# Denser idle products, eight packed first rows, and first-query banks copied whole by ScalarE with their rotation later

## The chip, the cores and the metric

The kernel runs on one core of a Trainium2 chip. It is timed by the device time of one execution, in microseconds; the time before the change is the median of three runs. TensorE is called PE here, its weight loads PEld, VectorE DVE, ScalarE ACT, GpSimd POOL, and SyncE, which issues most of the transfers, SP. L221 means line 221 of the kernel before.

## The reference, cut to what matters

One layer of an encoder on 256 tokens of width 2048, in float32. Only the first projection and the differential attention that reads it are touched by the change:

```python
h = rms_norm(x, norm_mix_pre[l])
proj = jnp.einsum('bsd,dc->bsc', h, w_in[l])
qa, ka, va, qn, kn, vn, gates = jnp.split(proj, split_at, axis=-1)
qa = apply_rope(qa.reshape(B, S, DA_HEADS, 2, DA_HEAD_DIM), cos, sin)
ka = apply_rope(ka.reshape(B, S, DA_HEADS, 2, DA_HEAD_DIM), cos, sin)
...
oa = diff_attention(qa, ka, va, lam)
```

After it come a neighbourhood attention, gates, an output projection and a squared-ReLU MLP of width 8192, which take up most of the time and which the change leaves as they are.

## The kernel before

**Numbers in two parts.** Each float32 operand is split in a high part, rounded to the type float32r that PE multiplies in one pass, and a low part, the rest. ACT makes the high part with a cast or a copy, DVE the low part with a subtraction (`split`, L137 and L143 for the casts, L145 for the subtraction). `wgroup` multiplies the high part of a weight tile with both parts of the activations (a product of 512 columns: 256 tokens high, 256 low; L221), and its low part with the high tokens alone (256 columns, L223). `agroup` takes three products of 512 columns for the same (L264 to L266).

**Groups.** The 2048 rows of `w_in` are 16 row tiles of 128, taken in four chunks of four. A group is 512 columns of `w_in`: four PSUM banks of 128 columns each for queries and keys (`wgroup`, one bank for each `b`), two banks for values (`agroup`). The first three groups are qa (queries), ka (keys) and va (values) of the first half of the heads. The eight banks of PSUM are two pools of four; qa, ka and va take theirs in turn from the same four, so bank `b` of ka can start only when bank `b` of qa has been read, and va needs the first two of ka.

**The start.** Four tiles `near` hold one row of the weights and of the transposed x each, side by side in a packed host array `front`, one transfer for each. The products of chunk 0 are issued row by row: four high ones, then four low ones (`k_first`). Chunks 1 to 3 come as pairs of rows, `first_w` and `xT` in turn, with casts and subtractions of two rows at a time; their products are left to the scheduler. `x_part` (L304, L305) scales the transposed x by the gains of the norm and splits it into `hT`. Before the data there are nine products of ones with ones into a bank that nobody reads (L171).

**The end of a query group.** `rope_evac` takes a bank by `halves`: ACT copies the right half (L289, to `rope_r`), DVE adds the left half of the bank to it (L291, to `rope_s`). Then DVE rotates with four more instructions and two products with the tables in `pack` (`cosT`, `sinT`; L432 to L435), ACT casts the high part (L418) and DVE subtracts for the low one (L419).

**The scale of the rows.** The projection is taken of x times gains, and the factor 1/rms of each token comes later. `second(ch)` runs between the chunks of ka: it loads four tiles of x in rows, ACT squares them and sums (L339, eight instructions), DVE and POOL make `rx` of the sums (L345, L98, L103), DVE puts it on a diagonal (`rxb_d`, L90), PE spreads it over the partitions (L91), ACT copies the result to `rxb` (L92), and DVE multiplies it into the tables (L349, L350). From there on rotated keys carry the factor.

**What sets the order.** A scheduler places the instructions of each engine by its own model of time, under the dependencies and the orders that `issue_after` adds; each engine then works through its list in that order. Transfers are issued by SP in order, at most eight under way at a time, since the ninth waits for the first. Weight tiles rotate through three buffers each for raw, high and low; a transfer into a raw buffer waits until the tile before in it has been split.

Of the kernel before, what the change touches and what calls it, by code (L numbers as in the profile page):

```python
# [17 lines left out]
P = 128  # L18
# [11 lines left out]
NMM = 4  # L30

# [19 lines left out]
def encoder_layer(ctx: ExitStack, tc: tile.TileContext, a, out):  # L51
# [55 lines left out]
    last_load = [None]  # L107
    front = []
    scaled = [None]

    def load(src, k0, nk, c0, cw, name):

        raw = wp.tile([P, nk, cw], F32, tag="raw", name=f"{name}_w")
        view = src[k0 * P : (k0 + nk) * P, c0 : c0 + cw].rearrange("(k p) c -> p k c", p=P)
        last_load[0] = nc.sync.dma_start(raw, view).ins
        return raw

    def split(raw, name, pieces=2, after=(), then=None):
# [7 lines left out]
        for s in range(pieces):  # L126
# [14 lines left out]
            with tc.issue_after(front[0]) if listed else nullcontext():  # L141
                if listed:
                    front[0] = nc.scalar.copy(hi[part], src).ins  # L143
                with tc.issue_after(front[1]) if then else nullcontext():
                    sub = nc.vector.tensor_sub(lo[part], src, hi[part].bitcast(F32)).ins  # L145
                if then:
                    front[1] = sub
# [7 lines left out]
    near = [page([P, (0 if k else KD) + 512 + T], F32, f"near{k}") for k in range(4)]  # L155
# [12 lines left out]

    idle = bank("idle")
    for i in range(9):  # L170
        nc.tensor.matmul(idle[:, :P], ones, ones, start=True, stop=True)  # L171

    xT = [None] + [page([P, 4, T], F32, f"xT{i}") for i in range(1, 4)]
# [38 lines left out]
    def wgroup(src, c0, act, nk, evac, name, first=(), hook=None, mid=None, after={}, k_first=False, inner=None):  # L212
# [14 lines left out]
        for ch in range(nk // 4):  # L227
# [3 lines left out]
            if ch < len(first):  # L231
                w = split(
                    first[ch], f"{name}_{ch}", 4 if k_first and ch == 0 else 2,
# [4 lines left out]
            if k_first and ch == 0:  # L238
# [47 lines left out]
    def halves(ps, name):  # L286

        r = t1k(f"{name}_r")
        act = nc.scalar.copy(r, ps[:, T:]).ins  # L289
        s = t1k(f"{name}_s")  # L290
        halved.extend((act, nc.vector.tensor_add(s, ps[:, :T], r).ins))  # L291
# [7 lines left out]
    def x_part(k):  # L299

        src = xT[k // 4][:, k % 4] if k > 3 else near[k][:, 512:]
# [27 lines left out]
    def x_rows(i):  # L329
        xt = page([P, 2, 512], F32, f"x_{i}")  # L330
        nc.sync.dma_start(
            xt, a["x"].rearrange("(t p) c -> p t c", p=P)[:, :, i * 512 : (i + 1) * 512]
        )
        xp.append(xt)
# [53 lines left out]
    halved = []  # L388
# [10 lines left out]
    def second(ch):  # L399
        if ch == 1:  # L400
            late[1] = halved[:8]
        if ch == 2:
            for i in range(4):
                x_rows(i)
# [22 lines left out]

    def rope_evac(dst):
        def evac(b, ps):
            s = halves(ps, "rope")  # L430
            u = t1k("rope_u")
            nc.vector.tensor_mul(u[0:64], s[64:128], sinT[64:128])  # L432
            nc.vector.tensor_mul(u[64:128], s[0:64], sinT[0:64])
            nc.vector.tensor_mul(s, s, cosT)
            nc.vector.tensor_add(s, s, u)  # L435
            parts(dst, (slice(None), b), s)
# [181 lines left out]
    for kind in ("a", "n"):  # L618
        for half in range(2):
# [6 lines left out]
            wgroup(w_in, qc + off, hmov, KD, qev(qT), f"q{nm}", **(head if nm == "a0" else {}))  # L626
            wgroup(w_in, kc + off, hmov, KD, kev(kT), f"k{nm}", **(head_k if nm == "a0" else {}))
            agroup(w_in, vc + off, hstat, KD, v_evac(v), f"v{nm}")
# [742 lines left out]
def _host_arrays(inputs):  # L1371
# [34 lines left out]
    w = arr["w_in"][: 4 * P, QA : QA + 512].reshape(4, P, 512)  # L1406
    arr["front"] = np.concatenate(
        [f["norm_mix_pre"][0].reshape(KD, P).T]
        + [part for k in range(4) for part in (w[k], arr["xT"][:, k])],
# [20 lines left out]
```

## Time and profile before

| | |
|---|---|
| median of three runs | 1341.35 us (1341.18 to 1341.43) |
| profiled execution, its own time | 1341.7 us |
| its span, first to last instruction | 1339.9 us |
| instructions | 16240 |
| granted PE clock over the span | 0.998 |
| first product on real data | 5.14 us after the span's start |
| first product of the key group ka | 28.70 us |
| first product of the value group va | 52.19 us |

Rows of the timeline give start, duration, engine, line, operation, output and inputs, shapes and a count; rows that follow each other alike are merged. What stands in brackets is how long the engine had been idle and what ended it. A PE row shows the whole way of a product through the array, so that rows overlap: the distance of two starts is what a product costs.

### The profile page before, as it was taken

How to read it: one execution, taken by the hardware profiler on the slowest of the kernel's cores; microseconds unless marked ns; L12 is line 12 of the kernel's file. 1: busy time of each engine (PE TensorE's matmuls, PEld its weight loads, DVE VectorE, ACT ScalarE, POOL GpSimd, SP SyncE). 2: the span in 40 equal slices, each digit the busy share in tenths (PEclk: the TensorE clock that was granted, in tenths of full speed). 3: DMA queues.
4: the chain of work that ended last, by engine and by line, in shares of the span. 5: the costliest groups of instructions: out<-in, count | busy, mean ns of one | idle time of the engine just before them, and what ended most of it. 6: DMA issues, size and time to landing. Idle time of an engine off the chain costs nothing.

```text
span 1339.9 us, 16240 instructions
## 1 busy us (share of the span) xinstructions
PE 1328.2 (99%) x6306; PEld 1112.9 (83%) x6306; DVE 1076.7 (80%) x1246; ACT 732.3 (55%) x864; POOL 38.5 (3%) x71
## 2 busy tenths in 40 slices
PE   9999999999999999999999999999999999999997
PEld 8888888888888888888888888888888888888885
DVE  7978866667777887655788999999988988898886
ACT  6655555544545554444476666666555555555542
POOL 0000000000000000000100000000000000000000
PEclk9999999999999999999999999999999999999999
DMA  9874655564565656575658777877797998698995
GB/s 343 277 219 161 197 166 179 184 186 157 188 220 171 209 192 209 199 277 188 223 187 275 239 249 277 294 237 249 250 360 291 401 374 336 247 372 333 354 355 201
DMA packets 116028, 335.85 MB, mean 251 GB/s; under 512 B 16752, under 2 KB 17008, under 8 KB 115952
## 3 DMA queue, kind: packets, MB, share of 16 engines
q1 hardware_dynamic: 96560, 266.13, 58.3%
q10 hardware_dynamic: 12672, 43.00, 8.3%
q0 software_dynamic: 6720, 25.69, 4.9%
q8 instruction: 49, 0.80, 0.2%
q14 instruction: 27, 0.22, 0.0%
HBM read 307.01 MB, written 29.61 MB: 251 GB/s over the span
## 4 chain that ended last, share of the span: by engine, by line
PE 96%; DMA 1%; DVE 1%; ACT 0%; SPq 0%; issue 0%; DVEq 0%; POOLq 0%; POOL 0%; ACTq 0%
PE u L740 25%; PE p L740 24%; PE ga L740 6%; PE gb L740 6%; PE ba L740 3%; PE bb L740 3%; PE qn_p L221 2%; PE kn_p L221 2%; PE y_p L266 2%; PE y_p L265 2%; PE y_p L264 2%; PE ka_p L221 2%; PE qn_p L223 1%; PE kn_p L223 1%; PE qa_p L221 1%; PE vn_p L264 1%
## 5 line engine op out<-in xcount | busy, mean ns | idle before, releaser
L145 DVE TENSOR_TENSOR y_l<-y_w,y_h 128x1024 fp32r<-128x1024 f32 x32 | 37.9, 1222 | 30.3 <-ACT y_h L137 30.3
L137 ACT CAST y_h<-y_w 128x1024 fp32r<-128x1024 f32 x32 | 32.0, 1051 | 40.1 <-PE y_p L266 32.5
L264 PE MATMUL y_p<-y_h,mh 128*128 128x512 f32 x128 | 50.1, 391 | 0.0
L265 PE MATMUL y_p<-y_l,mh 128*128 128x512 f32 x128 | 49.9, 390 | 0.0
L266 PE MATMUL y_p<-y_h,ml 128*128 128x512 f32 x128 | 49.8, 390 | 0.0
L221 PE MATMUL qn_p<-hT,qn_h 128*128 128x512 f32 x128 | 45.9, 400 | 0.0
L221 PE MATMUL ka_p<-hT,ka_h 128*128 128x512 f32 x128 | 45.4, 399 | 0.3 <-DVE rope_s L291 0.3
L221 PE MATMUL kn_p<-hT,kn_h 128*128 128x512 f32 x128 | 45.4, 398 | 0.0
L221 PE MATMUL qa_p<-hT,qa_h 128*128 128x512 f32 x128 | 43.6, 399 | 0.7 <-DVE hT L305 0.7
L740 PE MATMUL u<-u_2h,h2T 128*128 128x512 f32 x128 | 44.0, 396 | 0.0
L740 PE MATMUL u<-u_1h,h2T 128*128 128x512 f32 x128 | 43.4, 390 | 0.0
L740 PE MATMUL u<-u_4h,h2T 128*128 128x512 f32 x128 | 43.2, 391 | 0.0
L740 PE MATMUL u<-u_7h,h2T 128*128 128x512 f32 x128 | 41.0, 389 | 0.0
L740 PE MATMUL u<-u_6h,h2T 128*128 128x512 f32 x128 | 41.0, 389 | 0.0
L223 PE MATMUL qn_p<-hT,qn_l 128*128 128x256 f32 x128 | 35.9, 281 | 0.0
L223 PE MATMUL kn_p<-hT,kn_l 128*128 128x256 f32 x128 | 35.7, 280 | 0.0
L223 PE MATMUL ka_p<-hT,ka_l 128*128 128x256 f32 x128 | 35.2, 281 | 0.0
L223 PE MATMUL qa_p<-hT,qa_l 128*128 128x256 f32 x128 | 32.4, 281 | 0.3 <-DVE qa_l L145 0.3
L221 PEld LDWEIGHTS ka_p<-hT,ka_h 128*128 128x128 f32 x128 | 23.8, 188 | 6.0 <-DVE rope_s L291 0.7
L221 PEld LDWEIGHTS qn_p<-hT,qn_h 128*128 128x128 f32 x128 | 24.1, 188 | 5.3
L221 PEld LDWEIGHTS kn_p<-hT,kn_h 128*128 128x128 f32 x128 | 24.0, 188 | 5.3
L740 PEld LDWEIGHTS u<-u_1h,h2T 128*128 128x128 f32 x128 | 24.0, 188 | 5.0
(1473 smaller groups left out, 4422.2 us busy)
## 6 DMA issues: line engine op xcount, KB each, us to landing
y_w<-in_w_out SPq DMA_DIRECT2D x16, 1024.0 KB, 5.3
bh<-keeph ACTq DMA_DIRECT2D x30, 512.0 KB, 9.3
bl<-keepl ACTq DMA_DIRECT2D x30, 512.0 KB, 11.0
keeph<-ah POOLq DMA_DIRECT2D x18, 512.0 KB, 3.7
keepl<-al POOLq DMA_DIRECT2D x18, 512.0 KB, 7.1
va_w<-in_w_in SPq DMA_DIRECT2D x8, 1024.0 KB, 5.2
qn_w<-in_w_in SPq DMA_DIRECT2D x8, 1024.0 KB, 5.1
kn_w<-in_w_in SPq DMA_DIRECT2D x8, 1024.0 KB, 5.1
```

Of the source, the lines that this page charges most:

```text
L137: nc.scalar.copy(hi[part], src)
L145: sub = nc.vector.tensor_sub(lo[part], src, hi[part].bitcast(F32)).ins
L221: nc.tensor.matmul(ps[b], hi[:, k % 4, cs], mv, start=(k == 0), stop=False)
L223: nc.tensor.matmul(ps[b][:, :T], lo[:, k % 4, cs], mv[:, :T], start=False, stop=(k == nk - 1))
L264: nc.tensor.matmul(ps[t], sh, hi[:, k % 4], start=(k == 0), stop=False)
L265: nc.tensor.matmul(ps[t], sh, lo[:, k % 4], start=False, stop=False)
L266: nc.tensor.matmul(ps[t], sl, hi[:, k % 4], start=False, stop=(k == nk - 1))
L740: ins = nc.tensor.matmul(self.ps[i], st, mv[:, blk], start=i not in self.begun, stop=last and n == 2).ins
```

## The change

It has three parts. The idle products read a tile `warm` that DVE fills, in float32r and 512 columns wide, ten of them. Eight rows instead of four are packed into `front` and taken row by row (`NEAR`), and the transfers of chunk 1 fall away. The banks of the first queries (qa of the first half alone) are copied whole by ACT to four tiles `rope_c`; the add of the halves and the rotation are put into a list `rotations`, from which `second` takes two each at chunks 2 and 3 of ka, behind the low part of the last split so far. The casts of ka's chunk 1 are ordered behind these copies instead of behind the eight instructions of `halves`, and the loads of va behind the x rows.

```diff
+NEAR = 8
@@ load @@
-        last_load[0] = nc.sync.dma_start(raw, view).ins
+        with tc.issue_after(rows_load[0]) if rows_load[0] else nullcontext():
+            last_load[0] = nc.sync.dma_start(raw, view).ins
@@ split @@
+                last_low[0] = sub
...
-    near = [page([P, (0 if k else KD) + 512 + T], F32, f"near{k}") for k in range(4)]
+    near = [page([P, (0 if k else KD) + 512 + T], F32, f"near{k}") for k in range(NEAR)]
...
+    warm = page([P, 512], F32R, "warm")
+    nc.vector.memset(warm.bitcast(F32), 1.0)
     idle = bank("idle")
-    for i in range(9):
-        nc.tensor.matmul(idle[:, :P], ones, ones, start=True, stop=True)
+    for i in range(10):
+        nc.tensor.matmul(idle, warm[:, :P], warm, start=True, stop=True)
...
-    first = [[n[:, :512] for n in near]]
-    for i in range(1, 4):
+    first = [[n[:, :512] for n in near[i : i + 4]] for i in range(0, NEAR, 4)]
+    for i in range(NEAR // 4, 4):
@@ wgroup @@
-            if k_first and ch == 0:
+            if k_first and ch < NEAR // 4:
@@ second @@
         if ch == 1:
-            late[1] = halved[:8]
+            late[1] = copied
+        if ch > 1:
+            for _ in range(2):
+                rotations.pop(0)()
@@
+    def rope(dst, b, s):
+        u = t1k("rope_u")
+        nc.vector.tensor_mul(u[0:64], s[64:128], sinT[64:128])
+        nc.vector.tensor_mul(u[64:128], s[0:64], sinT[0:64])
+        nc.vector.tensor_mul(s, s, cosT)
+        nc.vector.tensor_add(s, s, u)
+        parts(dst, (slice(None), b), s)
...
+    def rope_late(dst):
+        def evac(b, ps):
+            c = t2k(f"rope_c{b}")
+            copied.append(nc.scalar.copy(c, ps.rearrange("p (a b) -> p a b", a=2)).ins)
+
+            def rest():
+                s = t1k("rope_s")
+                with tc.issue_after(last_low[0]):
+                    nc.vector.tensor_add(s, c[:, 0], c[:, 1])
+                rope(dst, b, s)
+
+            rotations.append(rest)
+
+        return evac
...
+            q_evac = rope_late(qT) if nm == "a0" else qev(qT)
```

The lists of the engines change in three places that the prediction speaks of. The first is DVE's list from the last split of the first keys' chunk 0 (`ka_0`) on; `qa_p` are banks of the first queries, `ka_n_l` low parts of chunk n of ka. Before:

```order
L145 TENSOR_TENSOR ka_0_l<-first_k_w,ka_0_h 128x1024 x2
L291 TENSOR_TENSOR rope_s<-qa_p_146,rope_r 128x256
L432 TENSOR_TENSOR rope_u<-rope_s,pack 64x256
L433 TENSOR_TENSOR rope_u<-rope_s,pack 64x256
L291 TENSOR_TENSOR rope_s<-qa_p_147,rope_r 128x256
```

With the change:

```order
L149 TENSOR_TENSOR ka_0_l<-first_k_w,ka_0_h 128x1024 x2
L149 TENSOR_TENSOR ka_1_l<-ka_1_w,ka_1_h 128x1024 x2
L463 TENSOR_TENSOR rope_s<-rope_c_326 128x256
L149 TENSOR_TENSOR ka_2_l<-ka_2_w,ka_2_h 128x1024
L441 TENSOR_TENSOR rope_u<-rope_s,pack 64x256
L442 TENSOR_TENSOR rope_u<-rope_s,pack 64x256
L463 TENSOR_TENSOR rope_s<-rope_c_336 128x256
```

Both subtractions of ka's chunk 1 now stand ahead of the first rotation, which reads ACT's copy and no bank. The second place is ACT's list between the casts of ka's chunk 2 and the end of the squares (`jx` are the squares, `x_...` the rows of x, `le` the exponentials of lambda, `qa` the high part of a rotated query). Before:

```order
L137 CAST ka_2_h<-ka_2_w 128x1024 x2
L418 CAST qa_140<-rope_s 128x256
L339 ACTIVATE jx_516,ssx<-x_467 128x512
L339 ACTIVATE jx_518,ssx<-x_467 128x512
L418 CAST qa_140<-rope_s 128x256
L339 ACTIVATE jx_520,ssx<-x_469 128x512
L339 ACTIVATE jx_522,ssx<-x_469 128x512
L137 CAST ka_3_h<-ka_3_w 128x1024 x2
L339 ACTIVATE jx_524,ssx<-x_471 128x512
```

With the change:

```order
L141 CAST ka_2_h<-ka_2_w 128x1024 x2
L141 CAST ka_3_h<-ka_3_w 128x1024 x2
L429 CAST qa_145<-rope_s 128x256 x2
L346 ACTIVATE jx_525,ssx<-x_458 128x512
L346 ACTIVATE jx_527,ssx<-x_458 128x512
L429 CAST qa_145<-rope_s 128x256
L346 ACTIVATE jx_529,ssx<-x_460 128x512
L429 CAST qa_145<-rope_s 128x256
L346 ACTIVATE jx_531,ssx<-x_460 128x512
L346 ACTIVATE jx_533,ssx<-x_462 128x512
```

All four casts of rotated queries now stand among the first squares, where before the last of them stood behind all eight. The third place is DVE's list at the change from keys to values (`va_n_l` are low parts of va's chunk n, `ka_p` banks of the keys). Before:

```order
L357 TENSOR_REDUCE ls<-lv 128x2
L145 TENSOR_TENSOR va_0_l<-va_0_w,va_0_h 128x1024
L90 TENSOR_SCALAR rxb_d_538<-ident,rx 128x128
L90 TENSOR_SCALAR rxb_d_541<-ident,rx 128x128
L348 TENSOR_SCALAR rxs<-rx 128x2
L145 TENSOR_TENSOR va_0_l<-va_0_w,va_0_h 128x1024
L419 TENSOR_TENSOR qa_141<-rope_s,qa_140 128x256
L360 SCALAR_TENSOR_TENSOR lam<-le 128x1
L145 TENSOR_TENSOR va_1_l<-va_1_w,va_1_h 128x1024 x2
L291 TENSOR_TENSOR rope_s<-ka_p_385,rope_r 128x256
```

With the change:

```order
L364 TENSOR_REDUCE ls<-lv 128x2
L367 SCALAR_TENSOR_TENSOR lam<-le 128x1
L91 TENSOR_SCALAR rxb_d_547<-ident,rx 128x128
L91 TENSOR_SCALAR rxb_d_550<-ident,rx 128x128
L355 TENSOR_SCALAR rxs<-rx 128x2
L298 TENSOR_TENSOR rope_s<-ka_p_358,rope_r 128x256
L149 TENSOR_TENSOR va_0_l<-va_0_w,va_0_h 128x1024 x2
L356 TENSOR_TENSOR pack<-pack,rxb 128x256
L357 TENSOR_TENSOR pack<-pack,rxb 128x256
L149 TENSOR_TENSOR va_1_l<-va_1_w,va_1_h 128x1024
L441 TENSOR_TENSOR rope_u<-rope_s,pack 64x256
L442 TENSOR_TENSOR rope_u<-rope_s,pack 64x256
```

The low parts of va's first two chunks moved behind the row scale and the first key bank. On PE the two products of the row scale (`rxb_p`) moved from the middle of ka's chunk 3 to its end; SP's list is the same but for the packed rows and one small input that is issued two transfers later. Some DVE and ACT instructions of the down projection trade places with a neighbour.

More of the change, by code (lines that the diff above doesn't have):

```diff
@@ L107, in encoder_layer @@
     last_load = [None]
+    last_low = [None]
+    rows_load = [None]
     front = []
@@ L232, in wgroup @@
                 w = split(
-                    first[ch], f"{name}_{ch}", 4 if k_first and ch == 0 else 2,
+                    first[ch], f"{name}_{ch}", 4 if k_first and ch < NEAR // 4 else 2,
                     then=(lambda k: x_part(ch * 4 + k)) if k_first else None,
@@ L299, in x_part @@
     def x_part(k):
-        src = xT[k // 4][:, k % 4] if k > 3 else near[k][:, 512:]
+        src = xT[k // 4][:, k % 4] if k >= NEAR else near[k][:, 512:]
         d = hT[k // 2][:, k % 2]
@@ L387, in encoder_layer @@
     first_k = []
-    halved = []
+    rotations = []
+    rows = []
     def tables():
```

33 lines of the change are left out of this document (15 added, 18 removed).

## Prediction

> **What bounds the kernel now.** I read the page's busy times and its chain first, then the list of who waits for whom on TensorE (PE), then the timeline of the first 75 us.
>
> ```profile
> PE 1328.2 (99%) x6306; PEld 1112.9 (83%) x6306; DVE 1076.7 (80%) x1246; ACT 732.3 (55%) x864; POOL 38.5 (3%) x71
> ...
> PE 96%; DMA 1%; DVE 1%; ACT 0%; SPq 0%; issue 0%; DVEq 0%; POOLq 0%; POOL 0%; ACTq 0%
> ```
>
> ```profile
> PE idle L171 <- POOL ones L163: 1.0, 1, 1.0
> PE qa_p L221 <- DVE hT L305: 0.7, 2, 0.5
> PE qa_p L223 <- DVE qa_l L145: 0.3, 1, 0.3
> PE ka_p L221 <- DVE rope_s L291: 0.3, 1, 0.3
> ```
>
> PE sets the end, and these are all its waits in 1340 us (total, times, longest). The change keeps every real product, so it can only remove what these waits cost and must not make new ones. The timeline (start, duration, engine) gives their price, because a pipelined PE row hides part of a wait.
>
> ```profile
> 5.14 1.17 PE L221 MATMUL qa_p<-hT,qa_h 128*128 128x512 f32 x4 [0.51 <-DVE hT L305]
> ...
> 8.01 1.09 PE L221 MATMUL qa_p<-hT,qa_h 128*128 128x512 f32 x4
> 8.94 0.63 PE L223 MATMUL qa_p<-hT,qa_l 128*128 128x256 f32 x4
> 9.41 1.09 PE L221 MATMUL qa_p<-hT,qa_h 128*128 128x512 f32 x4
> ...
> 11.14 1.19 PE L221 MATMUL qa_p<-hT,qa_h 128*128 128x512 f32 x4 [0.17 <-DVE hT L305]
> ...
> 12.68 0.39 PE L223 MATMUL qa_p<-hT,qa_l 128*128 128x256 f32 x1 [0.34 <-DVE qa_l L145]
> ...
> 28.70 0.40 PE L221 MATMUL ka_p<-hT,ka_h 128*128 128x512 f32 x1
> ...
> 32.94 0.86 PE L221 MATMUL ka_p<-hT,ka_h 128*128 128x512 f32 x3
> 34.11 0.50 PE L221 MATMUL ka_p<-hT,ka_h 128*128 128x512 f32 x1 [0.31 <-DVE rope_s L291]
> 34.44 0.28 PE L223 MATMUL ka_p<-hT,ka_l 128*128 128x256 f32 x1
> ```
>
> The wait at 5.14 is for the first transfer and stays. An undisturbed row of the weights (four high, four low products) takes 9.41 - 8.01 = 1.40 us, its four high ones 0.93 (0.233 each). So 11.14 is 9.41 + 1.40 + **0.33**; 12.68 is 11.14 + 0.93 + **0.61**; 34.11 is 32.94 + 3 x 0.233 + 0.47, and the product behind it starts 0.10 late: **0.57**. All that the change can save is 0.33 + 0.61 + 0.57 = 1.51 us, 0.11% of the run.
>
> **Idle products.** Ten float32r products of 512 columns replace nine float32 ones of 128 (two passes each), and wait for a DVE memset instead of POOL's.
>
> ```profile
> 0.74 0.20 POOL L163 MEMSET ones<- 128x128 f32 x1 [0.29 <-POOLq L1420]
> ...
> 1.00 2.72 PE L171 MATMUL idle<-ones 128*128 128x128 f32 x11 [1.00 <-POOL ones L163]
> ...
> 4.02 0.61 PE L171 MATMUL idle<-ones 128*128 128x128 f32 x4
> ```
>
> Eleven passes take 2.72 us, 0.25 each, the last four 0.61, 0.15 each with one row's tail in both: PE's pace about doubles near 3.9 us, 2.9 after the first pass and before the real work at 5.14. No row shows a DVE memset of 128x512; bounds are 0.20 (POOL's, a quarter of the size) and 0.69 (DVE's two-input 128x512, below). I take 0.5, nearer to the row of the same engine and size: first idle product at 1.3, some six at twice 0.233 until 3.9, four at 0.233, end about 5.0. Cost 0; the ends are -0.1 and +0.2 us at 5.14. "VectorE: DVE Perf Modes" of the Trainium skill (Zero memsets can be issued as uint32) says that a memset takes a cycle per element whatever its type; at 0.96 GHz that is an estimate of 0.53 us, and the sum stays.
>
> **Packed rows.** The bytes ahead of each row are the same, and ScalarE's waits show them landing.
>
> ```profile
> 7.78 0.51 ACT L304 ACTIVATE hT<-near,near 128x256 fp32r<-128x256 f32 x1 [0.29 <-DMA near<-in_front]
> ...
> 8.84 0.69 DVE L145 TENSOR_TENSOR qa_l<-near,qa_h 128x512 fp32r<-128x512 f32 x1
> ...
> 9.11 1.05 ACT L137 CAST qa_h<-first_w 128x1024 fp32r<-128x1024 f32 x1 [0.31 <-DMA first_w<-in_w_in]
> ...
> 11.36 1.05 ACT L137 CAST qa_h<-first_w 128x1024 fp32r<-128x1024 f32 x1 [0.39 <-DMA first_w<-in_w_in]
> ```
>
> Between 7.78 and 9.11 land 512 KB, until 11.36 another 768 KB. A packed row is 384 KB: row 4 lands near 8.8, then 9.9, 11.0, 12.1. From 7.78 to the end of its low half at 9.53 row 3 needs 1.75 us. So row 4 is complete at 10.5, and PE wants it at 10.8; rows 5 to 7 at 11.7, 12.8, 13.9 against 12.2, 13.6, 15.0. Both waits of chunk 1 go: **-0.94 us** (at the ends 0 and -0.94; chunk 2's lows are then due with some 0.1 us to spare, which I leave in the range). The eight rows cost ScalarE and DVE a few more short instructions, each hidden in these leads.
>
> **Banks emptied by ScalarE.** Four 128x512 copies replace four 128x256 ones; DVE's add moves off the bank. Their price lies between the rows of half the size and of a 128x512 activation out of a bank:
>
> ```profile
> 28.11 0.37 ACT L289 COPY rope_r<-qa_p 128x256 f32<-128x256 f32 x1 [1.32 <-DVE rope_s L291]
> ...
> 71.50 0.69 ACT L459 ACTIVATE va<-va_p,rx 128x512 fp32r<-128x512 f32 x1 [0.73 <-PE va_p L266]
> ```
>
> I take 0.6, near the second, which has the size. The fourth copy starts when the q products end, at 27.8 (28.70 - 0.94 is the first k product). Bank 3 is wanted 3 x 4 x 0.35 = 4.2 us later: the third wait goes, **-0.57 us**. Behind this copy stand the casts of ka_1, from 28.4.
>
> **What is late next: the v group.** Its low weights were early only because DVE never paused:
>
> ```profile
> 27.60:49.80 22.20, 21.89 (x127) 18.86 (x126) 21.86 (x43) 17.54 (x36) 0.71 (x1) 1.00 0.96 322
> ```
>
> ```profile
> 25.32 2.36 DVE L145 TENSOR_TENSOR ka_l<-first_k_w,ka_h 128x1024 fp32r<-128x1024 f32 x2 [0.22 <-ACT ka_h L137]
> ...
> 27.60 0.42 DVE L291 TENSOR_TENSOR rope_s<-qa_p,rope_r 128x256 f32<-128x256 f32 x1
> ...
> 33.97 1.22 DVE L145 TENSOR_TENSOR ka_l<-ka_w,ka_h 128x1024 fp32r<-128x1024 f32 x1
> ...
> 47.53 2.35 DVE L145 TENSOR_TENSOR va_l<-va_w,va_h 128x1024 fp32r<-128x1024 f32 x2
> ...
> 52.19 0.40 PE L264 MATMUL va_p<-va_h,hT 128*128 128x512 f32 x1
> ...
> 54.92 0.39 PE L264 MATMUL va_p<-va_h,hT 128*128 128x512 f32 x1
> ```
>
> DVE is busy for 21.86 of 22.20 us (third busy figure of the window), and va_1's lows end at 49.88. Afterwards DVE pauses twice. First, both halves of ka_1_l now stand ahead of all rotations: DVE is done with ka_0 at 27.68 and waits for ka_1_h until 29.5, 1.8 us. Second, ScalarE's queue puts the casts of rotated queries ahead of the squares of x, and each needs DVE's last add of that rotation.
>
> DVE from 29.5 to the fourth rotation's last add: six subtractions at 1.13 (2.35 less 1.22) and 22 short ones at 0.40 (sixteen between 27.60 and 33.97), 6.8 + 8.8 = 15.6, so 45.1. Three squares are done by then.
>
> ```profile
> 40.49 0.64 ACT L339 ACTIVATE jx<-x 128x512 f32<-128x512 f32 x1
> ...
> 42.34 0.62 ACT L339 ACTIVATE jx<-x 128x512 f32<-128x512 f32 x1
> ...
> 43.80 0.16 DVE L345 TENSOR_REDUCE sx<-ssx 128x2 f32<-128x8 f32 x1
> ...
> 44.31 0.71 POOL L103 TENSOR_TENSOR rx<-rx_m,expo 128x2 f32<-128x2 f32 x1 [42.86 <-DVE rx_m L98]
> 45.53 0.48 DVE L90 TENSOR_SCALAR rxb_d<-ident,rx 128x128 f32<-128x128 f32 x2
> 45.99 1.22 DVE L145 TENSOR_TENSOR va_l<-va_w,va_h 128x1024 fp32r<-128x1024 f32 x1
> ```
>
> Cast 0.4, five squares at 0.62 (three take 42.34 - 40.49): 48.6; it was 43.0. DVE, with nothing else ahead in its queue, has waited 2.5 us. The row scale takes 45.02 - 43.80 = 1.2 to POOL's end, rxb_d and rxs 0.46, the first k bank's add 0.34: 50.75. Then va_0_l 2.3, two table products 0.7, va_1_l's first half 1.1, two short ones 0.9, its second half 1.2: **57.0 us**. PE meets that operand at its 20th v product, in the run of before at 52.19 + 19 x 0.228 (54.92 - 52.19 is twelve) = 56.5; without new waits now 55.0. Waits for va_0_l, va_1_l and the row scale come to 2.0 us together. Later low weights keep 1 us and more (va_2 is due after 63.5, done near 61), so nothing is added behind it.
>
> **Sum** against the profiled execution, 1341.7 us (span 1339.9): -0.94 - 0.57 + 2.0 = +0.5 us, 1342.2. The three runs' median, 1341.35, lies 0.35 below it, so I forecast 1341.9, between 1341.2 and 1342.8.
>
> **Late swaps.** The order differs again in the down products, by one DVE step of 1.2 to 2.3 us:
>
> ```profile
> L694 DVE TENSOR_TENSOR d080el<-d080t,d080eh x2: 1219/1220/1220, 1098.5 to 1101.8; 128x1024 fp32r<-128x1024 f32 x2
> ...
> L740 PE MATMUL p<-d080el,bh x4: 389/389/389, 1106.9 to 1108.9; 128*128 128x512 f32 x4
> ```
>
> The second half is done at 1103.0 and used from 1106.9; this lead of 3.9 us hides the swap. Without it the swap would cost at most 2.3 us a step.
>
> **Rivals.** (1) The gain stays. If DVE's short steps and ScalarE's squares run 2 us ahead of my chain, v never waits: 1341.35 - 1.5 = 1339.9. For it: some thirty estimated steps in a row, and a 5 to 7 us lead before. Against: both queue orders are fixed, and DVE had no slack.
> (2) The clock, ending slower. If the idle block does not bring the pace up by 5.14, real products run at half pace. Price: before, the change came 2.9 us after the first idle product; counted again from 5.14 that loses 1.45 us, and the v chain, which hangs on the fourth copy, moves with it: 1341.9 + 1.45 = 1343.4. It decides when the idle block starts too late to be counted by 3.9. For it: the memset. Against: the products follow each other without a gap. "TensorE: Matmul & The Clock Gate" of the Trainium skill (Part 1) has a free-running window of about 3.4 us that looks at activity, not at products; by it, denser products bring nothing and a later start can only lose. The trace agrees on the doubling, but 2.9 us is shorter than that window.
> (3) The packing does nothing, because row 4's transfer is no earlier: -0.57 + 2.0 = +1.4, 1342.8. Against: equal bytes ahead of it.
>
> **Numbers.** Forecast 0.50; rival 1 0.30 (1339.6 to 1341.2); rival 2 0.08; rival 3 or a longer v chain 0.10, of which 0.04 beyond 1344.0; something unseen and faster 0.02. Eight in ten lie between 1339.7 and 1343.4. A measurement can tell about 0.2% (2.7 us) from no change: faster by more 0.02, within it 0.92, slower by more 0.06.
>
> **What would show it.** In the list of waits the three lines of before are gone, and PE waits for va_l instead (and for rxb_d). The first k product starts near 27.8. The eighth square ends near 48.6, rows of va_l lie at 51 to 57. If the squares end by 46, rival 1 holds; if real products after 5.14 stand twice 0.233 apart, rival 2; if a wait for hT or qa_l stays near 11, rival 3. A new wait behind 60 us would make the forecast wrong in a way not listed.

## The result, and the profile after

The changed kernel takes **1343.61 us** (median of 22 runs, 1342.96 to 1344.62) against 1341.39 for the kernel before (22 runs): a ratio of 1.0017, 95% interval 1.0011 to 1.0022. It is slower by 2.2 us, and the text above forecast slower by 0.5. The profiled execution took 1343.41 us with a span of 1341.6, against 1341.7 and 1339.9 before; of the 2.2 us between the medians the two profiles show 1.7.

First the busy times of the changed kernel, then its list of waits on PE (total, times, longest).

```profile
PE 1329.0 (99%) x6298; PEld 1112.6 (83%) x6298; DVE 1075.9 (80%) x1249; ACT 733.9 (55%) x866; POOL 38.6 (3%) x71
```

```profile
PE idle L178 <- DVE warm L175: 1.5, 1, 1.5
PE va_p L272 <- DVE va_l L149: 1.2, 2, 0.7
PE rxb_p L92 <- DVE rxb_d L91: 0.4, 1, 0.4
```

PE is still what sets the end. The three waits of before, for hT, qa_l and rope_s, are gone; three new ones have come, two in the v group for va_l and one just ahead of it for rxb_d. The timeline of PE in the changed kernel gives their place and price:

```profile
1.46 4.37 PE L178 MATMUL idle<-warm 128*128 128x512 f32 x10 [1.46 <-DVE warm L175]
5.87 1.17 PE L228 MATMUL qa_p<-hT,qa_h 128*128 128x512 f32 x4
...
50.43 0.28 PE L230 MATMUL ka_p<-hT,ka_l 128*128 128x256 f32 x1
51.09 0.71 PE L92 MATMUL rxb_p<-rxb_d,ones 128*128 128x128 f32 x4 [0.38 <-DVE rxb_d L91]
51.78 0.47 PE L271 MATMUL va_p<-va_h,hT 128*128 128x512 f32 x1
52.93 0.50 PE L272 MATMUL va_p<-va_l,hT 128*128 128x512 f32 x1 [0.67 <-DVE va_l L149]
53.26 0.40 PE L273 MATMUL va_p<-va_h,hT 128*128 128x512 f32 x1
...
55.57 0.39 PE L271 MATMUL va_p<-va_h,hT 128*128 128x512 f32 x1
55.87 0.50 PE L272 MATMUL va_p<-va_l,hT 128*128 128x512 f32 x1
...
57.13 0.40 PE L271 MATMUL va_p<-va_h,hT 128*128 128x512 f32 x1
58.01 0.50 PE L272 MATMUL va_p<-va_l,hT 128*128 128x512 f32 x1 [0.48 <-DVE va_l L149]
```

Products of v stand 0.23 us apart; here the distances are 1.15, 0.30 and 0.88 where PE needs a new half of va_l, and the product behind each such wait follows 0.33 to 0.34 later. The last k product is issued at 50.43 and the first v product at 51.78, with only the four short passes for rxb between.

Cutting each profile at the first product of each group shows where the time went. All numbers are starts and distances of starts from the timelines; the last column is the start of PE's last instruction.

| us | first real product | q group | k group | v group, to the first scores | all the rest | last PE start |
|---|---|---|---|---|---|---|
| before | 5.14 | 23.56 | 23.49 | 21.77 | 1256.19 | 1330.15 |
| after | 5.87 | 22.43 | 23.48 | 23.81 | 1256.08 | 1331.68 |

The start lost 0.73, the q group won 1.13, the k group won nothing and the v group lost 2.04; PE's work behind 76 us takes as long as before. The k group hides two things. It won its wait for the bank, and lost about as much at its end: from the last low k product to the first v product there are 1.35 us, before 0.12 (52.07 to 52.19), where the passes for rxb stood earlier, inside the group.

DVE and ACT show why. In the window that the prediction used, DVE is busy for 16.78 of 22.20 us (third busy figure), against 21.86 before:

```profile
27.60:49.80 22.20, 22.20 (x130) 19.44 (x129) 16.78 (x34) 12.94 (x28) 0.00 (x0) 1.00 0.84 301
```

```profile
28.50 0.59 ACT L458 COPY rope_c<-qa_p 128x512 f32<-128x512 f32 x1 [0.80 <-PE qa_p L230]
28.98 3.90 ACT L141 CAST ka_h<-ka_w 128x1024 fp32r<-128x1024 f32 x4
...
45.05 0.41 ACT L429 CAST qa<-rope_s 128x256 fp32r<-128x256 f32 x1 [0.70 <-DVE rope_s L444]
...
48.74 0.62 ACT L346 ACTIVATE jx<-x 128x512 f32<-128x512 f32 x1
```

```profile
30.07 2.36 DVE L149 TENSOR_TENSOR ka_l<-ka_w,ka_h 128x1024 fp32r<-128x1024 f32 x2 [3.06 <-ACT ka_h L141]
...
45.38 0.43 DVE L444 TENSOR_TENSOR rope_s<-rope_s,rope_u 128x256 f32<-128x256 f32 x1
...
49.49 0.16 DVE L352 TENSOR_REDUCE sx<-ssx 128x2 f32<-128x8 f32 x1 [2.32 <-ACT jx L346]
...
51.22 0.42 DVE L298 TENSOR_TENSOR rope_s<-ka_p,rope_r 128x256 f32<-128x256 f32 x1
51.65 2.36 DVE L149 TENSOR_TENSOR va_l<-va_w,va_h 128x1024 fp32r<-128x1024 f32 x2
...
56.73 1.23 DVE L149 TENSOR_TENSOR va_l<-va_w,va_h 128x1024 fp32r<-128x1024 f32 x1
```

DVE pauses twice, for 3.06 us until ka_1's cast (which waits behind the fourth bank copy, and that for the last q product) and for 2.32 us until the eighth square. In both the next instruction of its list is one that waits, and what stands behind cannot pass it. va_1_l is done at 57.96.

### The profile page after: what moved, and what is told of

It is laid out like the page before. It is cut to its first block, busy times and chain, and to the rows that moved or that the text cites. A ratio compares the mean times of both kernels' runs of the same rounds, so it can differ in the third digit from the quotient of the medians.

```text
span 1341.6 us, 16232 instructions
## 1 busy us (share of the span) xinstructions
PE 1329.0 (99%) x6298; PEld 1112.6 (83%) x6298; DVE 1075.9 (80%) x1249; ACT 733.9 (55%) x866; POOL 38.6 (3%) x71
## 4 chain that ended last, share of the span: by engine, by line
PE 97%; DVE 2%; ACT 0%; issue 0%; POOL 0%; DVEq 0%; POOLq 0%; ACTq 0%
PE u L773 25%; PE p L773 24%; PE ga L773 6%; PE gb L773 6%; PE ba L773 3%; PE bb L773 3%; PE qa_p L228 2%; PE qn_p L228 2%; PE kn_p L228 2%; PE y_p L273 2%; PE y_p L272 2%; PE y_p L271 2%; PE qa_p L230 1%; PE qn_p L230 1%; PE kn_p L230 1%; PE ka_p L228 1%
## 5 line engine op out<-in xcount | busy, mean ns | idle before, releaser
L773 PEld LDWEIGHTS u<-u_7h,h2T 128*128 128x128 f32 x128 | 24.0, 188 | 5.0
```

Of the source, the lines that this page charges most:

```text
L773: ins = nc.tensor.matmul(self.ps[i], st, mv[:, blk], start=i not in self.begun, stop=last and n == 2).ins
```

## The experiments

Theory: the late rotation alone makes the result. Through it the chain of the low parts of v hangs on the end of the q group (last q product, fourth copy, ka_1's casts, DVE), so that whatever k wins, PE waits for va_l. Rivals: the packing or the idle block makes it, by the late start; the chain hangs on transfers; DVE has too much work in any order. The runs were made in four groups, each with the kernel before on the same chip; its medians were 1341.30, 1341.27, 1341.33 and 1341.48. Landings, starts and groups are those of one profiled execution of each kernel, the medians those of 5 to 22.

### Each part alone

The idle products alone (idle_only), the packing alone (pack_only), both without the third part (no_late), and the third part alone (late_only).

```diff
 idle_only: before, with
-        nc.tensor.matmul(idle[:, :P], ones, ones, start=True, stop=True)
+        nc.tensor.matmul(idle, warm[:, :P], warm, start=True, stop=True)
...
 pack_only: before, with
+NEAR = 8
...
 no_late: before, with both of these
 late_only: after, with four rows and the old idle products
-NEAR = 8
+NEAR = 4
...
```

> The kernel before with the ten dense idle products alone. Open is why the first packed row landed at 4.68 us in the changed kernel and at 3.95 before, so that the first real product stood at 5.87 and not at 5.14. Theory A (the longer rows of the packed array): nothing of that here, first landing near 3.95, first real product at 5.1 to 5.2, time within 0.3 us of before, 1341.4. Theory B (the idle block or its fill holds the start up): first real product at 5.6 to 5.9 and 1342.1. Theory C (the landing varies from execution to execution): landing anywhere from 3.9 to 4.7 in the profile, the time within 0.3 us of before. The three old waits of PE stay by all.

> The kernel before with eight packed rows alone; idle products, rotations and banks as before. Theory A (the longer rows of the array delay the first landing by 0.7 us): first row lands near 4.7, first real product near 5.85, the waits for hT and qa_l near 11 to 13 us are gone (-0.94), sum -0.2, 1341.2. Theory C: first row lands by chance between 3.9 and 4.7; over many executions the start costs some 0.3, sum -0.6, 1340.8. If neither start nor rows matter: 1340.5 (-0.94). Waits of PE in the v group: none, by all theories.

> The changed kernel without its third part: rotations of the first queries and their banks as before, packed rows and idle products as after. Theory (the late rotations make the v group's waits): no wait of PE for va_l or rxb_d, 1341.2 by theory A of the start, 1340.5 to 1340.8 by C; the difference to the changed kernel, 1343.6, is then 2.4 to 3 us and all of it the third part's. Rival (the packing moves DVE's chain and so the v group): waits for va_l stay, and the time is above 1342.5.

> The changed kernel's third part alone: banks copied by ScalarE and late rotations; four packed rows and the old idle products. The q group ends about 0.9 us later than with the packing, and the chain on DVE to va_l hangs on ka_1's casts behind the fourth copy. Theory (the late rotations cost the v group 2.0 us beside 0.4 for rxb_d, and save 0.57): 1341.4 - 0.6 + 2.4 = 1343.2, or down to 1342.3 if the later q group gives the chain 0.9 us more. Rival (it takes the packing too): no waits for va_l, 1340.8. First landing near 3.95 by theory A, 3.9 to 4.7 by C.

| us | median | ratio, 95% interval | first landing | first real product | q | k | v |
|---|---|---|---|---|---|---|---|
| idle_only | 1341.60 | 1.0001, 0.9992 to 1.0010 | 4.22 | 5.88 | 22.59 | 23.33 | 21.80 |
| pack_only | 1341.66 | 1.0001, 0.9992 to 1.0010 | 4.33 | 5.52 | 23.11 | 23.57 | 21.80 |
| no_late | 1341.10 | 0.9999, 0.9990 to 1.0008 | 4.35 | 5.70 | 22.34 | 23.85 | 21.77 |
| late_only | 1343.51 | 1.0016, 1.0007 to 1.0025 | 4.14 | 5.34 | 23.22 | 23.47 | 23.82 |

The third part alone gives the whole result, down to the v group's 23.82 us; without it nothing is lost. The k and v columns show the mechanism as well: the first scores come 47.29 us after the first k product in late_only and in the changed kernel alike, although the two differ in start, packing and idle block; before it was 45.26. The expected 1343.2 came out to 0.3 us, and the rival that it takes the packing too fell. No expectation for the start held fully: the first landing in idle_only, 4.22, is later than the 3.95 of before with the same transfers, and its first real product is late for another reason.

```profile
1.46 4.64 PE L173 MATMUL idle<-warm 128*128 128x512 f32 x10 [1.46 <-DVE warm L170]
5.88 1.15 PE L223 MATMUL qa_p<-hT,qa_h 128*128 128x512 f32 x4
```

```profile
4.66 0.60 ACT L143 CAST qa_h<-near 128x512 fp32r<-128x512 f32 x1
...
4.79 0.48 DVE L307 SCALAR_TENSOR_TENSOR hT<-near,hT 128x256 fp32r<-128x256 f32 x1 [3.38 <-ACT hT L306]
```

In idle_only (PE's rows, then ACT's and DVE's) the operands are ready at 5.27, and the idle block holds PE until 5.88. Yet the median moves by only 0.3 us, inside the interval, and its q group ends before that of before (28.48 against 28.70): a start that is 0.74 later only takes the place of the waits for hT and qa_l, which are gone from its list of waits, though all three expectations had them stay.

pack_only shows the same from the other side. Its waits near 11 to 13 us are gone, and it gains nothing: its first product is 0.38 later, and one wait comes up that the prediction had left in its range, for a low part of a later chunk:

```profile
23.60 0.28 PE L224 MATMUL qa_p<-hT,qa_l 128*128 128x256 f32 x1
24.17 0.39 PE L224 MATMUL qa_p<-hT,qa_l 128*128 128x256 f32 x1 [0.29 <-DVE qa_l L146]
```

no_late reaches k 0.65 us earlier than before and gives 0.36 of it back in the k group, where it waits for two banks (its rows below); its 1341.10 lies between the two expectations:

```profile
31.22 0.50 PE L224 MATMUL ka_p<-hT,ka_h 128*128 128x512 f32 x1 [0.23 <-DVE rope_s L294]
...
33.89 0.51 PE L224 MATMUL ka_p<-hT,ka_h 128*128 128x512 f32 x1 [0.30 <-DVE rope_s L294]
```

### The head of the chain

Two edits move ka_1's casts ahead of the fourth copy (cast3), or of the third and fourth (cast2); a third delays the last q product by a dose (idle18).

```diff
 cast3
-            late[1] = copied
+            late[1] = copied[:3]
 cast2
+            late[1] = copied[:2]
 idle18
-    for i in range(10):
+    for i in range(18):
```

> The changed kernel with ka_1's casts waiting for three of the four bank copies instead of four, so that they stand ahead of the fourth copy on ScalarE. Theory (the chain to va_l begins with DVE's pause for ka_1_h, behind the fourth copy, and that copy follows the last q product): DVE's pause of 3.06 us shortens by 0.8 to 1.2 us, everything on DVE up to va_1_l moves by as much, and with it the v group's waits: 1342.4 to 1342.8. Rival (the chain hangs on ka_1's landing, on x or on DVE's later work): 1343.6 within 0.3. The fourth copy is later by 1 to 3 us; bank 3 of k is wanted some 4.2 us after the last q product, so a wait of PE there of up to 0.5 us may take part of it back.

> The changed kernel with ka_1's casts behind two of the four copies. A second point on the line from four (1343.6) over three (1341.3). Theory (the chain hangs on ka_1_h; its transfer lands near 27, so that the casts can begin 0.3 to 0.6 us earlier than with three): 1340.8 to 1341.3, DVE's pause ahead of ka_1_l at 0.5 to 0.9 instead of 1.11 us. Rival (the third and fourth copy now come late enough for PE to wait for banks 2 and 3 of k): a wait of ka_p for ScalarE of 0.3 us and more, 1341.5 to 1342.5.

> The changed kernel with 18 idle products instead of ten: a dose. The eight more run at full pace, 0.233 us each, so the first real product stands near 7.7 and not 5.87. Theory (with packed rows and with the chain to va_l hanging on the last q product, nothing absorbs a late start any more): 1343.6 + 1.87 = 1345.5, all of it at the start and the v group's waits about as before. Rival (the chain hangs on transfers, whose times the idle block doesn't move): the v group's waits shrink by what the start costs, 1343.6 to 1344.2.

| us | median | ratio, 95% interval | first real product | q | k | v | last PE start |
|---|---|---|---|---|---|---|---|
| cast3 | 1341.26 | 1.0001, 0.9993 to 1.0010 | 5.46 | 22.36 | 22.85 | 22.89 | 1329.50 |
| cast2 | 1340.83 | 0.9995, 0.9986 to 1.0004 | 5.63 | 22.35 | 22.66 | see below | 1328.80 |
| idle18 | 1345.75 | 1.0033, 1.0020 to 1.0045 | 7.57 | 22.30 | 23.48 | 23.80 | 1334.42 |

The direction is as the theory has it, and cast3 is worth twice what was expected: 2.35 us. In the two profiles its first scores come 2.02 us earlier, and 0.48 of that is there at the first k product, from a start that is 0.41 earlier; from there to the first scores it takes 45.74 us instead of 47.29. DVE's rows of cast3:

```profile
28.59 2.36 DVE L149 TENSOR_TENSOR ka_l<-ka_w,ka_h 128x1024 fp32r<-128x1024 f32 x2 [1.11 <-ACT ka_h L141]
...
47.42 0.16 DVE L352 TENSOR_REDUCE sx<-ssx 128x2 f32<-128x8 f32 x1 [1.70 <-ACT jx L346]
...
54.66 1.23 DVE L149 TENSOR_TENSOR va_l<-va_w,va_h 128x1024 fp32r<-128x1024 f32 x1
```

The first pause is 1.11 us, 1.95 shorter (0.8 to 1.2 had been expected), the second 1.70, and va_1_l's second half starts 2.07 earlier. The fourth copy now stands at 32.09 and makes PE wait nowhere. One wait of PE for va_l is left, 0.5 us. In cast2 none is left at all; the whole list of waits is that of the idle block for its fill:

```profile
PE idle L178 <- DVE warm L175: 1.5, 1, 1.5
```

Its scheduler also took the first scores of the attention earlier, so that its v group can't be compared by the first score. Its first pause of DVE is 1.09 us, as in cast3 and not the 0.5 to 0.9 expected; the second is 0.82 instead of 1.70. Its gain over cast3 in the median, 0.4 us, is inside the intervals.

idle18 came out as the theory had it: q, k and v groups are those of the changed kernel to within 0.13 us, only moved by the 1.70 us of the later start, and the v group did not absorb any of it: from the first k product to the first scores it is 47.28 us again. In the profiled execution, 1346.14 us, another 1.2 us is lost behind 76 us, in a wait of 1.3 us for uT near 1006 us; this was not followed up. Two of the five runs, 1344.71 and 1344.74, are only 1.1 us above the changed kernel, so that the 2.1 us between the medians is rough.

### The second pause

Three edits put all squares ahead of the casts of rotated queries on ACT. In the first (sq_first) x's loads moved too; in the second (sq_after) they stay behind ka_3; the third is sq_after with `copied[:3]`.

```diff
 sq_after (casts of the rotations and of va issue after the squares)
+    def squares():
+        with tc.issue_after(last_load[0]):
+            rows = [x_rows(i) for i in range(4)]
+        for i in range(4):
+            x_squares(i)
+        for _ in range(4):
+            casts.pop(0)()
+        row_scales()
...
-    head_k = dict(hook=second, first=first_k, after=late)
+    head_k = dict(hook=second, mid=squares, first=first_k, after=late)
```

> The changed kernel, with ScalarE's queue in another order: the eight squares of x stand behind ka_3's casts, and the casts of the rotated queries and of va stand behind the squares. Same work. Theory (the waits of the v group come from DVE's pause for the squares, which stood behind casts that need a rotation's last add): squares end near 40.6, some 1.3 us behind the last x row, DVE's pause of 2.3 us ahead of sx is gone, PE has no wait for va_l or rxb_d, and the time falls by the 2.04 us that the v group lost and the 0.4 of rxb_d, to 1341.1. Rival 1 (DVE has too much work there whatever the order): waits for va_l stay above 1 us, 1342.6 or more. Rival 2 (the squares block ScalarE for the later x rows and va's casts come late): PE waits for va_h, 1342 to 1344.

> The run with the squares first, with its fault mended: there x's transfers had moved ahead of ka_2's in SP's queue, ka_2 landed at 35.6 us instead of 29.6 and DVE stood still for it. Here the x rows are loaded behind ka_3 again. All four copies still stand ahead of ka_1's casts. Theory (both pauses of DVE count; this takes out the second, 2.3 us ahead of sx, and lets va_0_l and va_1_l start under the rotations): no wait for va_l, at most 0.6 us for the first k bank's add, whose place on DVE is now behind va_1_l; 1341.0 to 1341.7. Rival (only the first pause counts, since what DVE doesn't do in the second it has to do anyway): the v group's waits shrink by less than 0.5 us, 1343.1 or more.

> Both: squares ahead of the late casts, x behind ka_3, and ka_1's casts ahead of the fourth copy. Theory: PE has no wait but that for the fill of the idle block; cast3's 1341.3 less the 1.1 us that its v group still loses (its first scores stand 22.90 us behind the first v product, against 21.77 before): 1340.2, faster than both kernels by about 0.1%. Rival (the first k bank's add, now behind four casts' subtractions and va_1_l on DVE, keeps va_p waiting): 1341 to 1342.

sq_first: 1346.56 us (1.0044, 1.0031 to 1.0056), slower by 2.95 than the changed kernel. It misses its question: the scheduler put x's transfers ahead of ka_2's, and ACT's row shows what followed.

```profile
35.70 2.00 ACT L143 CAST ka_h<-ka_w 128x1024 fp32r<-128x1024 f32 x2 [4.77 <-DMA ka_w<-in_w_in]
```

sq_after: 1342.41 us (1.0008, 0.9999 to 1.0017), 1.2 better than the changed kernel and not the 1.9 to 2.6 expected. Its list of waits has no va_l any more, but rxb_d in its place (the profiled execution, 1344.05 us, is one of the two longest of eleven, so that its rows show the place and not the price). PE's rows, then DVE's:

```profile
50.32 0.38 PE L92 MATMUL rxb_p<-rxb_d,ones 128*128 128x128 f32 x2
52.15 0.49 PE L92 MATMUL rxb_p<-rxb_d,ones 128*128 128x128 f32 x2 [1.45 <-DVE rxb_d L91]
```

```profile
48.87 0.28 DVE L91 TENSOR_SCALAR rxb_d<-ident,rx 128x128 f32<-128x128 f32 x1
...
49.14 2.35 DVE L151 TENSOR_TENSOR va_l<-va_w,va_h 128x1024 fp32r<-128x1024 f32 x2
...
51.82 0.28 DVE L91 TENSOR_SCALAR rxb_d<-ident,rx 128x128 f32<-128x128 f32 x1
```

The second half of rxb_d now stands behind va_1_l on DVE. With the casts moved too (sq_after_cast3) it is the add of the first k bank that stands there, PE waits 1.5 us for rope_s, and the time is 1342.67 (1.0010, 1.0001 to 1.0019): 1.4 worse than cast3 alone. The expected 1340.2 failed in the way that its rival names, though the time lies above that rival's 1341 to 1342 too. What the second pause is worth stays open: sq_after suggests that it counts, but all that these two runs show is that taking it out by an order which also moves DVE's list puts another short instruction of DVE behind a long one.

### The start, and what the packing is worth

Fewer idle products (idle7), cast3 with four packed rows (cast3_near4), cast2 with the packed rows in two arrays (cast2_two) and with the old idle block (cast2_old_idle).

```diff
 idle7
+    for i in range(7):
 cast3_near4
+NEAR = 4
 cast2_two
...
+        nc.sync.dma_start(n, a["front2" if k > 3 else "front"][:, at : at + n.shape[1]])
...
 cast2_old_idle
+    for i in range(9):
+        nc.tensor.matmul(idle[:, :P], ones, ones, start=True, stop=True)
```

> The changed kernel with seven idle products instead of ten, so that the block ends near 4.6 at half pace instead of 5.83. Theory (the block, not the first operands, holds the first real product up, by 0.1 to 0.6 us as the first row lands at 4.7 or at 3.95): first real product at 5.0 to 5.8, directly behind its operands; 1343.2 (1342.9 to 1343.5). Rival (the pace then doubles later than the start, since in the runs so far it came 3 to 4.2 us behind the first idle product, and real products run at half pace until then): four to eight real products 0.43 us apart, 1343.6 to 1344.

> cast3 with four packed rows instead of eight: what the packing is worth once the chain to va_l is short. Theory (packing is worth the waits for hT and qa_l, less what a start at 5.5 to 5.9 behind the idle block absorbs of them): q group 0.1 to 0.5 us longer than cast3's 22.36, 1341.4 to 1341.8. Rival (it is worth the predicted 0.94): 1342.2. Rival (nothing): 1341.3.

> cast2 with the eight packed rows in two arrays of four, so that a row of the first array is as long as before (12352 bytes a partition, not 24640); same transfers of the same sizes in the same order. Theory (the longer rows make the first transfer slower by about 0.33 us): first landing at 3.95 to 4.2 instead of 4.2 to 4.7; the first real product then stands behind the idle block, at 5.4 to 5.7, so that little of it reaches the time: 1340.6 (1340.4 to 1340.9). Rival (four more transfers, or chance): landing at 4.2 to 4.7, 1340.8.

> cast2 with the old idle block (nine products of 128x128 from POOL's ones), which ended at 5.0 to 5.2 in the runs with packed rows or late rotations alone. Theory (the dense block holds the first product up by 0.1 to 0.4 us, and the pace doubles no earlier for it): first real product directly behind its operands, at the first landing plus 1.2, 5.4 to 5.6; 1340.6 (1340.3 to 1340.9). Rival (the gap of 0.3 to 0.5 us between the old block and the first operands lets the pace fall back, as the gap of 1.1 us did behind seven dense products): real products at half pace for up to 2.7 us, 1341.5 to 1342.3.

| us | median | ratio, 95% interval | first landing | first real product | q |
|---|---|---|---|---|---|
| idle7 | 1345.12 | 1.0026, 1.0016 to 1.0036 | 4.69 | 5.89 | 23.85 |
| cast3_near4 | 1342.22 | 1.0005, 0.9996 to 1.0014 | 3.98 | 5.35 | 23.05 |
| cast2_two | 1340.66 | 0.9994, 0.9985 to 1.0003 | 4.08 | 5.89 | 22.36 |
| cast2_old_idle | 1340.73 | 0.9994, 0.9985 to 1.0003 | 4.22 | 5.42 | 23.04 |

idle7 is 1.5 us slower than the changed kernel, more than either theory had. The block ended at 4.81, the first real product came at 5.89, and behind that gap PE was still at half pace:

```profile
5.89 2.04 PE L228 MATMUL qa_p<-hT,qa_h 128*128 128x512 f32 x4 [1.08 <-DVE hT L312]
7.73 1.05 PE L230 MATMUL qa_p<-hT,qa_l 128*128 128x256 f32 x4
8.59 1.30 PE L228 MATMUL qa_p<-hT,qa_h 128*128 128x512 f32 x4
9.73 0.52 PE L230 MATMUL qa_p<-hT,qa_l 128*128 128x256 f32 x3
```

The next row of the weights starts 2.70 us behind the first, where an undisturbed one takes 1.40; the q group takes 23.85 us against 22.43, 1.42 more. Its k and v groups are those of the changed kernel (23.48 and 23.81). Two of the nine runs, 1342.84 and 1343.06, are 2 us below the other seven, so that they were probably spared this; they have no profile, and which of the landing and the pace differed in them is not shown.

cast3_near4 gives the worth of the packing in cast3: 1342.22 against 1341.26, 0.96 us between medians from two groups of runs. The two profiles show 0.70 at PE's last start, with a q group that is 0.69 longer. The expected 0.1 to 0.5 failed; the rival, the 0.94 of the prediction, fits the medians. cast2_two and cast2_old_idle are within 0.2 us of cast2: neither the longer rows nor the denser block matter for the time, since a later start removes waits of the q group (cast2_old_idle starts 0.47 earlier than cast2_two and has two waits, for hT and qa_l, and a q group that is 0.68 longer). The rival of cast2_old_idle fell: PE stood idle for 0.41 us between its idle block and its first real product, and its first real products stood 0.23 us apart all the same.

**The best version** is cast2 or either of its two variants, 1340.66 to 1340.83: 2.8 to 2.95 us below the changed kernel, and 0.5 to 0.8 below the kernel before. All three medians lie below that of the kernel before beside them, but each interval still holds 1, so that the second gain is likely rather than shown.

## Why the prediction was right and wrong

**Direction and mechanism** were right: the sum had the three waits gone, the v group late, and a small loss. In the list of waits the three old rows are gone and rows for va_l and rxb_d have come; va_l's rows lie at 51.65 to 57.96, where 51 to 57 was said; and both pauses of DVE are there. **The size** was wrong: +0.5 was predicted and +1.7 came between the two profiles, +2.2 between the medians (before's profile lay 0.35 us above the median on which the forecast was shifted, after's 0.2 below its own).

**The step that failed** is the start, which the sum put at nothing: "Idle products ... end about 5.0. Cost 0; the ends are -0.1 and +0.2 us at 5.14", and "The wait at 5.14 is for the first transfer and stays". The first real product came at 5.87, +0.73. Two things went another way. The first row landed at 4.68 instead of 3.95, as ACT's first rows show, before and after:

```profile
3.97 0.51 ACT L304 ACTIVATE hT<-near 128x256 fp32r<-128x256 f32 x1 [1.95 <-DMA near<-in_front]
```

```profile
4.70 0.51 ACT L311 ACTIVATE hT<-near 128x256 fp32r<-128x256 f32 x1 [2.68 <-DMA near<-in_front]
...
5.24 0.48 DVE L312 SCALAR_TENSOR_TENSOR hT<-near,hT 128x256 fp32r<-128x256 f32 x1 [3.84 <-ACT hT L311]
```

So the operands were ready at 5.72, and the first product followed 0.15 later, as in before (4.99 and 5.14). Why the row landed later stays open (last section). And the idle block did not end about 5.0. Its products ran 0.43 us apart until the ninth, which the tenth followed after 0.39:

```profile
5.04 0.55 PE L178 MATMUL idle<-warm 128*128 128x512 f32 x1
```

```profile
5.43 0.40 PE L178 MATMUL idle<-warm 128*128 128x512 f32 x1
```

With the 0.23 of the full pace behind 5.43 the block would have let PE go at 5.66, half a microsecond after 5.14. In the changed kernel the landing binds, in idle_only the block: with ten such idle products and operands at 5.27 the first real product stood at 5.88. In the eight other kernels with ten of them it stood between 5.35 and 5.89, never at 5.14. The doubling that the prediction read in before, 2.9 us after the first pass, was that of one execution: in pack_only the same eighteen passes keep the slow pace to their end. The block in before, then in pack_only:

```profile
1.00 3.64 PE L171 MATMUL idle<-ones 128*128 128x128 f32 x18 [1.00 <-POOL ones L163]
```

```profile
1.00 4.15 PE L172 MATMUL idle<-ones 128*128 128x128 f32 x18 [1.00 <-POOL ones L164]
```

How this ran through the working, by the landmarks that the prediction gave:

| us | predicted | measured |
|---|---|---|
| first real product | 5.14 | 5.87 |
| first k product | 27.8 | 28.30 |
| casts of ka_1 begin | 28.4 | 28.98 |
| DVE's first pause ends | 29.5 | 30.07 |
| last add of the fourth rotation ends | 45.1 | 45.81 |
| eighth square ends | 48.6 | 49.4 |
| add of the first k bank ends | 50.75 | 51.64 |
| va_1_l done | 57.0 | 57.96 |

Of the 0.96 us at the end of this chain 0.57 is there when DVE begins, and comes from the start; the thirty estimated durations behind it add 0.4 (0.55 counted from the terms themselves, which add up to 50.6 at the first k bank and not to 50.75). idle18 shows that a later start reaches the v group undiminished. The start alone does not account for the miss: without these 0.57 the estimate is 1343.61 - 0.57 = 1343.0, still 1.1 above the forecast. The rest is the 0.4, some 0.2 behind this chain, and 0.55 by which the two profiles lie on different sides of their medians.

**Packed rows, -0.94.** The landings were right (8.77, 9.74, 10.73, 11.70 for 8.8, 9.9, 11.0, 12.1), and the price fits cast3_near4. What failed is that it counted on a start of 5.14: a late start and the packing take away the same waits. idle_only, with four rows and a start at 5.88, has a q group of 22.59 us, only 0.16 longer than the changed kernel. So start and q group together gave -0.40 instead of -0.94. Nor does late_only's 1343.51, without packing, against 1343.61 show that the packing is swallowed later: late_only started 0.53 earlier, its q group was 0.79 longer, and the 0.26 that was left at the first k product is less than the medians can tell.

**Banks, -0.57.** The wait went, and counted without the passes for rxb the k products end 0.88 us sooner after the first of them than before (0.57 is the wait; the other 0.31 was not traced). The 2.0 us for the v group with rxb, the largest term, were 0.87 at the seam from k to v (1.35 less 0.48: the last product and the passes for rxb) and 2.04 inside the group, 2.9 in all: va_1_l ended 0.96 later than the 57.0 of the sum. The sum by measured terms is -0.40 - 0.88 + 2.91 = +1.63 where the profiles have +1.53 at PE's last start.

**Late swaps, hidden**: right, 1256.08 for 1256.19 us behind the first scores.

**Rivals.** (1), the gain stays, fell for this change, by the two pauses; in cast2, with the first one at 1.09 us and no wait left in the v group, the median lies 0.5 below before, not clear of noise and not the 1.5 of the rival. (2), the clock, did not happen in the changed kernel: from 5.87 on its rows are 1.4 us apart. But its price was right, 1.45 predicted and 1.42 measured in the q group of idle7. Its point of decision was not: the block of idle7 starts as in the changed kernel, and what differs is that it does not reach up to the operands. (3), the packing does nothing, fell by its mechanism, though pack_only's time looks like it: there the gain was lost to the start and to the next wait.

On the clock, "TensorE: Matmul & The Clock Gate" of the Trainium skill (Part 1) lets the change of pace vary with the phase of a free-running window, by half a microsecond either way. The traces agree that it varies and that the denser block gained nothing by its density, but they vary by more: the doubling came 2.9 us after the first idle pass in before, and, by the distances of the products, 3.2 to 5.1 us after it in the kernels with ten dense products; here the measurement decides. The same page (Why this matters for your kernels) warns of idle gaps above some 3 us. The gap in idle7 was 1.08 us and came before the pace had once doubled, so that it does not test this line; what its trace shows is that the pace doubled only near 9.0 us, 3.2 us after the first real product. Gaps of 0.28, 0.38 and 0.41 us (late_only, pack_only, cast2_old_idle) were followed by products 0.30 and then 0.23 us apart.

## What to carry to other kernels

Where a second engine's chain begins at the end of one group and ends behind the next, only what moves its beginning or shortens it reaches the time: in the changed kernel, late_only, idle18 and idle7, which share the late rotation as it is, the first scores came 47.3 us after the first k product, whatever stood before. The wait for the bank lay beside that chain, and its removal was worth nothing. Two savings that take away the same waits don't add up either: the late start had taken most of what the packing was to save. A deferred piece of work should be looked at from the queue into which it is put: here the copies that freed the banks stood in front of the casts that feed the next engine, and with one copy behind those casts the kernel took 2.35 us less, some 0.5 of it by an earlier start. An idle block has to end close to the first operands (0.28 to 0.41 us of idle time did no harm here, 1.08 cost 1.5 us in the time), and each product beyond that costs its own time once nothing later absorbs it.

## What the runs showed of the hardware

The landing of the first transfer, issued at 0.74 us in every kernel, varies from profile to profile: 3.95, 3.98, 4.14 and 4.22 with four rows in the packed array, 4.21 to 4.69 (mean 4.38) in eleven profiles with eight rows and the longer stride, 4.08 with eight rows in two arrays. This suggests that the stride makes the difference of some 0.3 us; with one profile for each kernel it is not shown.

PE's pace doubled near 3.9 us of the span in before and between 4.7 (cast3_near4) and 6.5 (sq_after_cast3) in the others, idle7 apart, and not at the same point for the same work: idle18 and idle_only issue the same ten products from 1.46 on, and the tenth was followed after 0.27 us in the one and after 0.42 in the other.
